# Retention transposes three half units behind the norm, output weights fetched a unit sooner, low parts first in batch 1, x2 stored in column halves

## The chip, the cores and the metric

The kernel runs on one core of a Trainium2 chip. The core has five engines, each with its own instruction stream, run in order: TensorE (PE: matrix products and transposes into PSUM), VectorE (DVE), ScalarE (ACT), GpSimd (POOL) and SyncE (SP), which here issues the DMA transfers between HBM and the on-chip memory. Semaphores tie the streams together. The metric is the time of one execution on the device, in microseconds (us); less is better.

## The reference

One layer of a hybrid encoder runs over two inputs of 512 rows by 1024 columns, "batch 0" and "batch 1" here. Everything is float32:

```python
mod = silu(c) @ w_ada + b_ada                      # sh1, sc1, g1, sh2, sc2, g2
h = rms_norm(x, norm1_g) * (1 + sc1) + sh1
q_a, k_a, v_a, q_r, k_r, v_r, g_r = split(h @ w_in)
o_a = windowed_attention(q_a, k_a, v_a, sink)      # 8 heads of 64, blocks of 128 rows
o_r = bidirectional_retention(q_r, k_r, v_r, g_r)  # 4 heads of 128
x = x + g1 * (concat(o_a, o_r) @ w_out)
h = rms_norm(x, norm2_g) * (1 + sc2) + sh2
x = x + g2 * (square(relu(h @ w_mlp1)) @ w_mlp2)
return rms_norm(x, final_g)
```

Retention normalises each head's output y before it is gated: the mean is taken off, the result is multiplied by 1/sqrt(variance + 1e-6) and by silu(g_r).

## The kernel before

**Precision.** A float32 matrix is split into a high part that TensorE multiplies at full rate and a low part, the rest. A product is three matmuls: high·high, high·low, low·high. The high part is a cast on ScalarE, the low part a subtraction on VectorE. A weight w becomes the tiles `wh_…` and `wl_…`. For batch 0 weights are loaded, split and also written back to HBM (`keep_unit`); batch 1 loads the two parts (`kept_unit`): the high ones into pool `ws`, the low ones of the output weights into pool `ws2`, which has 3 slots and also takes parts of the MLP's weights (`wc_a`, `wc_s`).

**Units.** The work on TensorE is a list of units, one per weight tile. `run_units` loads a unit's weights while the unit before it computes; after each half unit it calls `between(rate)`. This gives the waiting stages (attention blocks, retention heads) `rate` steps of credit. A stage is a generator; `yield n` says that its next step may not come before n half units. Two stages are active at a time.

**Retention.** `ret_head` computes the scores `prs` of a 128-row chunk, multiplies them with the decay mask (`rsf`, VectorE), splits them (`rsc`), and multiplies them with the values into `py`. Then y is transposed into `pyn`, VectorE takes mean and variance (`mv`), `va` = variance + eps (tile `rva`) and `nb` = −mean (`rnb`), GpSimd raises `rva` to −1/2 (`rrs`) and multiplies `rnb` by it, ScalarE writes the normalised `ryn`, and four transposes give `pyb`, which is gated into `mix`.

**Output projection.** `out_units(b)` makes eight units: column half `hf` (512 columns) times four parts `kq` of the inner dimension (two 128-blocks each). A half's four row tiles t build up in four banks `po_b_hf_t`. The mixer's output is split into `ms` when the weights of half 0 are loaded. `mm3_late` takes the products of a unit so that those with the weight's low part come last. At part 3 each row tile is finished by itself: product with the gate row (`go`), addition to x (`x_b_t`); for half 0 of batch 1 the tile of x is loaded there, in program order. After half 1 the row is complete: `store` writes it to `x2s`, `squares` (ScalarE) and `scaled` (VectorE, GpSimd) make the second norm; for batch 1 the last row tile is scaled into two tiles `xl_0`, `xl_1`. `norm2` transposes the scaled rows into `px_b_kc` (the transposes are at line 268). The MLP then follows (`py_…`, `px_…` at line 940 with the weights `wc_…` and the halves of its input `hch`, `hcl`).

**Order around the change.** Batch 1's units (attention, values, four retention heads) run at rate 1.3; then `out_units(0)` by itself at rate 1.0, with its first weights loaded when its first unit begins; then batch 1's output projection beside `norm2` of batch 0 and the first MLP products. A scheduler orders the engines' streams from the recorded program; SyncE's queue is served in order, so a transfer whose semaphore isn't there holds all behind it.

## Time and profile before

| | us |
|---|---|
| median of 3 runs | 1107.09 |
| lowest, highest | 1106.03, 1108.5 |
| profiled execution, its own time | 1107.0 |
| its span | 1105.2 |
| mean granted TensorE clock | 0.998 |

The profile gives, for one execution, when each instruction ran and which semaphore ended a wait. "Busy" matmuls overlap each other, so the duration of one (0.39 us for 512 columns) is longer than the distance from one to the next. An engine that is busy for nearly the whole span sets its length; what the others do matters where that engine waits for them.

### The profile page before, as it was taken

The numbers are of one execution on the slowest core, as the hardware profiler recorded it, in microseconds if no ns is written. First come the engines' busy times: TensorE is split into PE (matmuls) and PEld (weight loads), VectorE is DVE, ScalarE is ACT, GpSimd is POOL, SyncE is SP. The second block draws the span as 40 slices with busy tenths as digits, with TensorE's granted clock in tenths as the row PEclk, the third lists the DMA queues.
The fourth block names the chain that finished last, engine by engine and source line by source line (L and its number), as shares of the span: only waits on it lengthen the run. The fifth ranks groups of instructions, "written<-read, shape, count | busy, mean of one in ns | idle before, by whom it ended". The sixth has DMA issues, their size and how long they took to land.

```text
span 1105.2 us, 14046 instructions
## 1 busy us (share of the span) xinstructions
PE 1081.8 (98%) x5021; PEld 889.3 (80%) x5021; DVE 864.2 (78%) x1448; ACT 516.0 (47%) x885; POOL 53.3 (5%) x63
## 2 busy tenths in 40 slices
PE   8999999999999999999999999999999999999997
PEld 5777887777888787888888888888888888888886
DVE  7979898877885787789778777786759754589786
ACT  6576676545652443474433333333443732335342
POOL 1000000010000001000000000000000000002213
PEclk9999999999999999999999999999999999999999
DMA  9888898855545698633555445552883555525504
GB/s 373 336 303 314 303 346 271 248 179 175 171 156 180 229 362 302 256 146 126 190 181 184 159 152 176 169 190 105 300 325 109 187 192 196 206 77 191 190 20 152
DMA packets 86746, 232.73 MB, mean 211 GB/s; under 512 B 8578, under 2 KB 20882, under 8 KB 86676
## 3 DMA queue, kind: packets, MB, share of 16 engines
q1 hardware_dynamic: 86084, 231.25, 60.3%
q8 instruction: 39, 0.64, 0.2%
q10 hardware_dynamic: 432, 0.57, 0.1%
q14 instruction: 31, 0.25, 0.1%
q0 software_dynamic: 160, 0.02, 0.0%
HBM read 160.75 MB, written 71.06 MB: 210 GB/s over the span
## 4 chain that ended last, share of the span: by engine, by line
PE 82%; DVE 11%; ACT 2%; DMA 2%; issue 1%; POOL 1%; POOLq 0%; DVEq 0%; ACTq 0%
PE x L1357 16%; PE px_None L940 15%; PE y L1357 12%; PE py_None L940 11%; PE po L132 2%; PE po L134 2%; PE po L131 2%; DVE jka_b L178 2%; PE po L396 2%; PE ppt L389 1%; PE psc L360 1%; PE pj_rq L131 1%; PE pj_rq L132 1%; PE pj_rq L134 1%; DVE jka_f L178 1%
## 5 line engine op out<-in xcount | busy, mean ns | idle before, releaser
L1297 DVE TENSOR_TENSOR uc_l<-ur,uc_h 128x1024 fp32r<-128x1024 f32 x56 | 68.4, 1221 | 52.7 <-ACT uc_h L1297 35.5
L1357 PE MATMUL x<-wc_l,uc_h 128*128 128x512 f32 (+1 forms) x264 | 101.0, 383 | 0.0
L1357 PE MATMUL x<-wc_h,uc_l 128*128 128x512 f32 (+1 forms) x264 | 101.0, 383 | 0.0
L1357 PE MATMUL x<-wc_h,uc_h 128*128 128x512 f32 (+1 forms) x264 | 100.9, 383 | 0.0
L1297 ACT CAST uc_h<-ur 128x1024 fp32r<-128x1024 f32 x56 | 58.8, 1051 | 77.1 <-PE x L1357 25.1
L1357 PE MATMUL y<-wc_h,uc_h 128*128 128x512 f32 x192 | 74.7, 389 | 0.0
L1357 PE MATMUL y<-wc_l,uc_h 128*128 128x512 f32 x192 | 74.7, 389 | 0.0
L1357 PE MATMUL y<-wc_h,uc_l 128*128 128x512 f32 x192 | 74.7, 389 | 0.0
L1297 ACT CAST wc_h<-w 128x1024 fp32r<-128x1024 f32 x48 | 50.5, 1051 | 48.1 <-PE x L1357 24.7
L1297 DVE TENSOR_TENSOR wc_l<-w,wc_h 128x1024 fp32r<-128x1024 f32 x48 | 58.6, 1220 | 17.6 <-ACT wc_h L1297 13.6
L1357 PEld LDWEIGHTS x<-wc_h,uc_h 128*128 128x128 f32 x264 | 49.6, 188 | 9.9 <-issue 0.2
L1357 PEld LDWEIGHTS x<-wc_l,uc_h 128*128 128x128 f32 x264 | 49.6, 188 | 9.7
L1357 PEld LDWEIGHTS x<-wc_h,uc_l 128*128 128x128 f32 x264 | 49.6, 188 | 9.6
L131 PE MATMUL po<-wh_wo,ms 128*128 128x512 f32 x128 | 50.3, 397 | 0.0
L132 PE MATMUL po<-wh_wo,ms 128*128 128x512 f32 x128 | 49.8, 392 | 0.1
L178 DVE CUSTOM_DVE_ANT_0 jka_b<-raw_adat,cb,cols 128x1024 bf16<-128x1024 f32 x38 | 48.3, 1280 | 0.2
L845 ACT CAST wc_s4h<-raw_w 128x1024 fp32r<-128x1024 f32 x16 | 16.8, 1052 | 63.1 <-PE px_None L940 44.9
L370 ACT ACTIVATE st<-st,negm 128x256 f32<-128x256 f32 (+1 forms) x64 | 35.2, 554 | 20.1 <-DVE negm L365 20.1
L1357 PEld LDWEIGHTS y<-wc_h,uc_h 128*128 128x128 f32 x192 | 36.0, 188 | 7.5
L1357 PEld LDWEIGHTS y<-wc_l,uc_h 128*128 128x128 f32 x192 | 36.0, 188 | 7.5
L1357 PEld LDWEIGHTS y<-wc_h,uc_l 128*128 128x128 f32 x192 | 36.0, 188 | 7.5
L940 PE MATMUL py_None<-hch,wc_a 128*128 128x512 f32 x120 | 39.7, 389 | 0.0
(379 smaller groups left out, 2963.0 us busy)
## 6 DMA issues: line engine op xcount, KB each, us to landing
ur<-spill SPq DMA_DIRECT2D x56, 512.0 KB, 4.4
raw_adat<-in_w_ada_t_dram SPq DMA_DIRECT2D x36, 512.0 KB, 6.4
raw_w<-in_w_mlp_dram SPq DMA_DIRECT2D x32, 512.0 KB, 3.5
spill<-s SPq DMA_DIRECT2D x64, 256.0 KB, 3.6
w<-in_w_mlp_dram SPq DMA_DIRECT2D x32, 512.0 KB, 5.0
spill<-u SPq DMA_DIRECT2D x48, 256.0 KB, 2.0
raw_ada<-in_w_ada_t_dram SPq DMA_DIRECT2D x12, 512.0 KB, 9.3
x<-in_x_dram SPq DMA_DIRECT2D x12, 512.0 KB, 7.7
```

The source lines that it names most:

```text
L131: nc.tensor.matmul(ps, lhs[0], rhs[0], start=start, stop=False)
L132: nc.tensor.matmul(ps, lhs[late], rhs[1 - late], start=False, stop=False)
L134: nc.tensor.matmul(ps, lhs[1 - late], rhs[late], start=False, stop=stop)
L178: nc.vector.tensor_tensor_reduce(junk(f"jka_{name}_{sec}_{kc}_{b}"), t, cb[:, b, :], 1.0, bcol[:, sec * KC + kc:sec * KC + kc + 1] if bias ...
L360: nc.tensor.matmul(psc[:, :w], qs[hh][:, isl], k_[:, s, j0 * P:j1 * P], start=(s == 0), stop=(s == 1))
L370: nc.scalar.activation(st[hh][:, :w], st[hh][:, :w], AF.Exp, bias=negm[:, hh:hh + 1], scale=0.125, accum_out=den[:, hh:hh + 1])
L389: nc.tensor.transpose(pt[:, hh * P:(hh + 1) * P], st[hh][:, jj * P:(jj + 1) * P], ident)
L396: nc.tensor.matmul(po, va[:, j0 + jj, g].rearrange("p s e -> p (s e)"), pts[jj][:, s, :], start=(jj == 0 and s == 0), stop=(jj == nj - 1 a ...
L845: nc.scalar.copy(hi, src)
L940: self.last = nc.tensor.matmul(bank[:, cs], x[:, k, :], y, start=first and k == 0 and i == 0, stop=last and k == 3 and i == 2, skip_group_ ...
L1297: last_split[:] = [nc.scalar.copy(hi, src), nc.vector.tensor_sub(lo, src, f(hi))]
L1357: nc.tensor.matmul(out, left[n][x][:, i, ts_], right[n][y][:, i, cs], start=first and i == 0 and k == 0, stop=end and i == 1 and k == 2, s ...
```

## The change

The edits are these. `mm3_late` can take the products with the weight's low part first, and does so for batch 1's output projection. In `ret_head`, `nb` is computed ahead of `va`, and the transposes into `pyb` come three half units behind the norm instead of two. `store` takes a column range; batch 1 stores each half of a row as soon as it is added. `out_units(0)` is appended to batch 1's units in one list, so the load of its first weights falls beside the last retention unit, and its half units give 1.3 steps, not 1.0.

```diff
-    def mm3_late(groups, late):
+    def mm3_late(groups, late, low_first=False):
+        def low():
+            for ps, lhs, rhs, start, stop in groups:
+                nc.tensor.matmul(ps, lhs[1 - late], rhs[late], start=start and low_first, stop=stop and not low_first)
+        if low_first:
+            low()
+        for ps, lhs, rhs, start, stop in groups:
+            nc.tensor.matmul(ps, lhs[0], rhs[0], start=start and not low_first, stop=False)
+            nc.tensor.matmul(ps, lhs[late], rhs[1 - late], start=False, stop=stop and low_first)
+        if not low_first:
+            low()
...
         va = small([P, NT], f"rva_{nm}")
-        nc.vector.tensor_scalar(va, mv[:, :, 1], EPS, None, ALU.add)
         nb = small([P, NT], f"rnb_{nm}")
         nc.vector.tensor_scalar(nb, mv[:, :, 0], -1.0, None, ALU.mult)
+        nc.vector.tensor_scalar(va, mv[:, :, 1], EPS, None, ALU.add)
...
-        yield 2
+        yield 3
         pb = aux_bank(f"pyb_{nm}")
...
-        def store(t):
+        def store(t, cs=slice(0, D)):
             r0 = b * S + t * P
-            nc.sync.dma_start(x2s[r0:r0 + P, :], x2[t])
+            nc.sync.dma_start(x2s[r0:r0 + P, cs], x2[t][:, cs])
...
-                               (w[0][:, k, :], w[1][:, k, :]), kq + k == 0, kq + k == 4) for t in ts_ for k in range(2)], 1)
+                               (w[0][:, k, :], w[1][:, k, :]), kq + k == 0, kq + k == 4) for t in ts_ for k in range(2)], 1, b == 1)
...
+                        if b == 1:
+                            store(t, hs)
                         if hf == 1 and b == 1:
-                            store(t)
                             squares(hf, t)
...
-    run_units(units, 1.3)
-    units, norm2_0 = out_units(0)
-    run_units(units, 1.0)
+    more, norm2_0 = out_units(0)
+    run_units(units + more, 1.3)
```

How the streams change at three places. First VectorE at the norm of retention head 2 of batch 0 (`mv_2` is its mean and variance, `jka_b` a piece of the modulation, `qs` the low part of an attention projection). Before:

```order
L453 TENSOR_SCALAR rva_2_2333<-mv_2_2320 128x4
L338 TENSOR_TENSOR qs_0_2306<-pj_q_0_2267,qs_0_2306 64x512
L178 ISA jka_b_6_0_2313,gm<-raw_adat_2218,cb,cols 128x1024
L178 ISA gm 128x1
L455 TENSOR_SCALAR rnb_2_2335<-mv_2_2320 128x4
L178 ISA jka_b_6_1_2362,gm<-raw_adat_2218,cb,cols 128x1024
L178 ISA gm 128x1
L422 SCALAR_TENSOR_TENSOR rsf_3_2_2371<-prs_3_2_2367,dtab_3_2186 128x512
L467 SCALAR_TENSOR_TENSOR mix_3_1841<-pyb_2_2397,rg_2_1838 128x512
```

With the change:

```order
L456 BN_AGGR mv_2_2315<-bn_2_3_2325 128x2
L459 TENSOR_SCALAR rnb_2_2329<-mv_2_2315 128x4
L460 TENSOR_SCALAR rva_2_2328<-mv_2_2315 128x4
L427 SCALAR_TENSOR_TENSOR rsf_3_1_2344<-prs_3_1_2340,dtab_3_2190 128x512
L430 TENSOR_TENSOR rsc_3_1_2346<-rsf_3_1_2344,rsc_3_1_2346 128x512
L183 ISA jka_b_6_1_2366,gm<-raw_adat_2222,cb,cols 128x1024
L183 ISA gm 128x1
L343 TENSOR_TENSOR qs_1_2380<-pj_q_1_2353,qs_1_2380 64x512
```

`rnb_2` stood four rows behind `rva_2`; now the two are neighbours.

Second TensorE at the beginning of batch 0's output projection, which falls beside head 2 of batch 1 (`prs_2_3`: scores of its chunk 3; `py_2<-rsc_2_1`: chunk 1 times its values; `po_0_t`: the projection's banks). Before, from `prs_2_2` on:

```order
L124 MATMUL prs_2_2_3923<-rq_2_3531,rk_2_3602 128x512
L125 MATMUL prs_2_2_3923<-rq_2_3531,rk_2_3602 128x512
L126 MATMUL prs_2_2_3923<-rq_2_3531,rk_2_3602 128x512
L124 MATMUL py_2_3814<-rsc_2_1_3845,rv_1_2868 128x512
L131 MATMUL po_0_0_3904<-wh_wo_0_0_3879,ms_0_0_3883 128x512
L131 MATMUL po_0_1_3905<-wh_wo_0_0_3879,ms_0_0_3883 128x512
L131 MATMUL po_0_2_3906<-wh_wo_0_0_3879,ms_0_0_3883 128x512
L131 MATMUL po_0_3_3907<-wh_wo_0_0_3879,ms_0_0_3883 128x512
L124 MATMUL prs_2_3_3949<-rq_2_3531,rk_2_3602 128x512
L125 MATMUL prs_2_3_3949<-rq_2_3531,rk_2_3602 128x512
```

With the change, the rows that end in the same product:

```order
L136 MATMUL po_0_1_3899<-wh_wo_0_1_3885,ms_1_1_3892 128x512
L137 MATMUL po_0_1_3899<-wh_wo_0_1_3885,ms_1_1_3892 128x512
L132 MATMUL po_0_0_3898<-wl_wo_0_1_3886,ms_1_0_3889 128x512
L132 MATMUL po_0_0_3898<-wl_wo_0_1_3886,ms_1_1_3892 128x512
L132 MATMUL po_0_1_3899<-wl_wo_0_1_3886,ms_1_0_3889 128x512
L132 MATMUL po_0_1_3899<-wl_wo_0_1_3886,ms_1_1_3892 128x512
L124 MATMUL py_2_3845<-rsc_2_1_3880,rv_1_2864 128x512
L125 MATMUL py_2_3845<-rsc_2_1_3880,rv_1_2864 128x512
L126 MATMUL py_2_3845<-rsc_2_1_3880,rv_1_2864 128x512
L124 MATMUL prs_2_3_4003<-rq_2_3526,rk_2_3594 128x512
```

Before, the product with `rsc_2_1` follows the last row of its scores `prs_2_1` after 18 matmuls and four transposes, and another chunk's scores are put between its parts; now 49 matmuls lie between, a whole half unit of the projection among them, and its three parts stand together.

Third SyncE's queue in batch 1's output projection (`x_1_t` is row tile t of x, `wh_wo_1_q` and `wl_wo_1_q` the weights of column half 1, part q, `raw_w` the MLP's weights). Before:

```order
L787 DMA x_1_0_4652<-in_x_dram 128x1024
L787 DMA x_1_1_4657<-in_x_dram 128x1024
L787 DMA x_1_2_4662<-in_x_dram 128x1024
L787 DMA x_1_3_4667<-in_x_dram 128x1024
L119 DMA wh_wo_1_1_4692<-kept_wo_1_4239 128x1024
L119 DMA wl_wo_1_1_4694<-kept_wo_1_4239 128x1024
L119 DMA wh_wo_1_2_4758<-kept_wo_2_4289 128x1024
L119 DMA wl_wo_1_2_4760<-kept_wo_2_4289 128x1024
L876 DMA raw_w_1_0_4921<-in_w_mlp_dram 128x1024
L253 DMA gate_1_512_4762<-gates 128x512
L119 DMA wl_wo_1_3_4809<-kept_wo_3_4353 128x1024
L119 DMA wh_wo_1_3_4807<-kept_wo_3_4353 128x1024
```

With the change:

```order
L740 DMA x2s<-x_1_0_4652 128x512
L792 DMA x_1_1_4658<-in_x_dram 128x1024
L119 DMA wl_wo_1_2_4764<-kept_wo_2_4324 128x1024
L882 DMA raw_w_1_0_4925<-in_w_mlp_dram 128x1024
L740 DMA x2s<-x_1_1_4658 128x512
L792 DMA x_1_2_4664<-in_x_dram 128x1024
L119 DMA wl_wo_1_3_4813<-kept_wo_3_4359 128x1024
L740 DMA x2s<-x_1_2_4664 128x512
L792 DMA x_1_3_4670<-in_x_dram 128x1024
L740 DMA x2s<-x_1_3_4670 128x512
L258 DMA gate_1_512_4766<-gates 128x512
L119 DMA wh_wo_1_3_4811<-kept_wo_3_4359 128x1024
```

The four loads of x stood together; now each of the last three stands behind the half store of the tile before, and the gate row and `wh_wo_1_3` behind all four stores. On TensorE, in the same place, the eight matmuls with `wl_wo_1_3` stood behind the high ones of each tile and are now ahead of them, and 24 rows of the MLP, where there were 8, stand between them and the sixteen with `wh_wo_1_3`.

More of the change, by code (lines that the diff above doesn't have):

```diff
@@ L126, in mm3 @@
         nc.tensor.matmul(ps, lhs[1], rhs[0], start=False, stop=stop)
-    def mm3_late(groups, late):
-        for ps, lhs, rhs, start, _ in groups:
-            nc.tensor.matmul(ps, lhs[0], rhs[0], start=start, stop=False)
-            nc.tensor.matmul(ps, lhs[late], rhs[1 - late], start=False, stop=False)
-        for ps, lhs, rhs, _, stop in groups:
-            nc.tensor.matmul(ps, lhs[1 - late], rhs[late], start=False, stop=stop)
+    def mm3_late(groups, late, low_first=False):
[9 more added lines that the diff above has]
+            low()
     ident = const.tile([P, P], F32, name="ident")
```

## The prediction

> **What bounds the kernel now.** I read the page first: the span, the engines' busy time, and the chain of work that ended last.
>
> ```profile
> span 1105.2 us, 14046 instructions
> PE 1081.8 (98%) x5021; PEld 889.3 (80%) x5021; DVE 864.2 (78%) x1448; ACT 516.0 (47%) x885; POOL 53.3 (5%) x63
> PE 82%; DVE 11%; ACT 2%; DMA 2%; issue 1%; POOL 1%; POOLq 0%; DVEq 0%; ACTq 0%
> ```
>
> TensorE is busy for 1081.8 of 1105.2 us and holds 82% of the chain. The change adds no matmul and takes none away, so it can win only where TensorE stands still and lose only where it will. The profiled execution took 1107.0 us, 1.8 around its span; the median of three runs is 1107.09, so both are the same to 0.1. The order of instructions differs between the two kernels only from TensorE's row for about 172 us to that for about 505 us. The table of busy time by stretch (columns: stretch, its length, then busy time of PE, PEld, DVE, ACT and POOL with their instructions, granted clock, DMA share, GB/s) gives what can be had there:
>
> ```profile
> 172.00:505.00 333.00, 325.85 (x1604) 268.17 (x1603) 266.07 (x579) 164.07 (x343) 18.29 (x25) 1.00 0.64 216
> 246.00:322.00 76.00, 75.61 (x384) 62.24 (x383) 60.85 (x182) 46.35 (x124) 0.00 (x0) 1.00 0.49 159
> 322.00:374.00 52.00, 52.00 (x239) 42.94 (x237) 34.58 (x76) 16.06 (x29) 2.41 (x4) 1.00 0.60 203
> 374.00:380.00 6.00, 4.87 (x19) 3.19 (x18) 6.00 (x12) 2.70 (x5) 0.00 (x0) 1.00 0.40 156
> 460.00:475.00 15.00, 14.29 (x67) 11.73 (x66) 14.52 (x25) 7.84 (x15) 0.00 (x0) 1.00 0.33 117
> 486.30:490.00 3.70, 2.48 (x22) 2.49 (x23) 2.60 (x5) 3.16 (x5) 0.00 (x0) 1.00 0.15 55
> ```
>
> 333.00 less 325.85 is 7.15 us of idle time at full clock, and that, with some slow spacing that counts as busy, is the most the change can win. The waits of TensorE name it (engine, tile, line, releaser: total, times, longest):
>
> ```profile
> PE pyb L466 <- ACT ryn L461: 3.1, 4, 1.3
> PE px L268 <- ACT x L749: 1.4, 1, 1.4
> PE py L124 <- ACT rsc L424: 1.0, 1, 1.0
> PE py L940 <- ACT wc_a L845: 0.7, 1, 0.7
> PE px L268 <- DVE x L751: 0.3, 1, 0.3
> PE ppt L389 <- DVE mx L362: 0.3, 1, 0.3
> ```
>
> **Retention transposes one half unit later, and −mean ahead of the variance.** The timeline at heads 2 and 3 of batch 0 (start, duration, instruction, idle before it and its releaser):
>
> ```profile
> 222.86 0.17 DVE L453 TENSOR_SCALAR rva<-mv 128x4 f32<-128x4 f32 x1
> 223.78 1.29 DVE L178 CUSTOM_DVE_ANT_0 jka_b<-raw_adat,cb,cols 128x1024 bf16<-128x1024 f32 x1
> 224.99 0.17 DVE L455 TENSOR_SCALAR rnb<-mv 128x4 f32<-128x4 f32 x1
> 225.31 1.10 POOL L459 TENSOR_TENSOR rnb<-rnb,rrs 128x4 f32<-128x4 f32 x1 [1.13 <-DVE rnb L455]
> 226.95 0.33 PE L466 MATMUL pyb<-ident,ryn 128*128 128x128 f32 x1 [1.04 <-ACT ryn L461]
> 244.00 1.38 PE L466 MATMUL pyb<-ident,ryn 128*128 128x128 f32 x4 [0.26 <-ACT ryn L461]
> 372.33 0.60 PE L466 MATMUL pyb<-ident,ryn 128*128 128x128 f32 x4
> ```
>
> At head 2 a low part and a modulation step got between the two small VectorE operations: `rnb` came 2.1 us behind `rva`, and GpSimd and ScalarE waited. In the changed order they are neighbours, and the matmuls between `pyn` and `pyb` grow from 27 to 31. The 1.04 us wait goes, with some 0.06 of spacing: 1.1. At head 3 the distance more than doubles; the wait of 0.26 goes, and the four transposes, which took 1.38 us at ScalarE's pace, take 0.60 as they do at 372.33: 1.0 together. **Gain 2.1.** Heads 0 and 1 of batch 0 keep exactly their old matmuls between `pyn` and `pyb`, by the order of both kernels, so the rest of the 3.1 us, 1.28 and 0.49 (1.8), stays. If the new cover failed, the two waits would stay: 0, and above 2.1 there is nothing there to win.
>
> In batch 1, head 3, the transposes slip behind `ms` halves that VectorE makes for the joined output units; one pair costs
>
> ```profile
> 444.92 1.29 DVE L768 TENSOR_TENSOR ms<-mix,ms 128x512 fp32r<-128x512 f32 x2
> ```
>
> and two of these stand ahead of `rnb`. They lie beside 6.1 us of matmuls, against 5.4 before, so between −0.5 and one full pair, 1.3: I take a **loss of 0.3**.
>
> **Output projection of batch 0 joined to batch 1's units.** At its start TensorE waited for the last scores of a chunk:
>
> ```profile
> 373.49 0.40 PE L124 MATMUL prs<-rq,rk 128*128 128x512 f32 x1
> 373.95 0.40 PE L126 MATMUL prs<-rq,rk 128*128 128x512 f32 x1
> 375.38 0.49 PE L124 MATMUL py<-rsc,rv 128*128 128x512 f32 x1 [1.03 <-ACT rsc L424]
> ```
>
> Two steps in 0.46 us make 0.23 for one 512-column matmul. The stretch from 374 to 380 holds 19 of them, 4.3 us of 6.0: 1.7 lost, where the wait itself shows 1.03. Before, the first `py` row for chunk 1 stood 18 matmuls and four transposes (4.5 us of work) behind the last `prs` row of its scores; in the changed kernel it stands 49 matmuls behind (11.3 us). The path between them is a mask product, a cast and a low part on two engines; the smallest such distance anywhere in the changed order is 6.1 us. **Gain 1.7** (bounds 1.0 and 2.0). The weights that are now fetched a unit sooner, and the casts, low parts and `ms` halves that go with them, fall into 322 to 374 us. There VectorE is busy for two thirds of the time and the DMA engines for 0.60; nothing in that stretch waits on either, so I cost the move at nothing. If that cover were gone, a unit's low parts would hold TensorE for one pair, 1.3.
>
> Stages of batch 1 also start sooner. The attention stretch from 246 to 322 us has 0.39 us idle and a 0.3 us wait of `ppt`; by the changed order no score is nearer to its use than 5.5 us. **Gain 0.6**, with bounds −1.0 (the three stalls that the nearer scores could bring, at 0.3) and 1.5. The wait of `px` for batch 0's scaled rows, 0.3, gets 0.9 us more matmuls ahead of it: **gain 0.3**, or none if the stores on which the scaling waits stay late.
>
> **Low parts first and stores by column halves, batch 1.** This is the part that can cost. Rows for the DMAs between 440 and 490 us (tiles, queue, count, size, median us from issue to landing), one from the page for half-size stores, and the end of the stretch in the chain of waits:
>
> ```profile
> x<-in_x_dram SPq DMA_DIRECT2D x4, 512.0 KB, 8.8
> raw_w<-in_w_mlp_dram SPq DMA_DIRECT2D x3, 512.0 KB, 4.1
> x2s<-x SPq DMA_DIRECT2D x4, 512.0 KB, 2.8
> wl_wo<-kept_wo SPq DMA_DIRECT2D x4, 512.0 KB, 7.4
> spill<-u SPq DMA_DIRECT2D x48, 256.0 KB, 2.0
> DMA to landing us min/median/max: 4.7/4.7/4.7
> 453.98 0.68 DVE L790 TENSOR_TENSOR x<-x,go 128x512 f32<-128x512 f32 x1
> 473.76 0.39 PE L940 MATMUL py<-hch,wc_a 128*128 128x256 f32 x1 [0.71 <-ACT wc_a L845]
> 480.04 1.22 DVE L846 TENSOR_TENSOR wc_s4l<-raw_w,wc_s4h 128x1024 fp32r<-128x1024 f32 x1
> 480.00 0.47 PE po L134 x2
> 482.50 3.71 DMA x2s<-x
> 486.31 1.16 ACT x L749
> 487.51 1.09 PE px L268 x8
> 488.61 1.44 PE px L940 x12
> ```
>
> (The row with 4.7 three times is that of `wh_wo_1_3`.) Now SyncE issues the four loads of x in a row; in the changed program each later load stands behind the store of the tile before, and that store waits for VectorE's addition. So loads 1 to 3 run one after the other. With 4.4 us for a load, between the 4.1 of `raw_w` and the 4.7 of `wh_wo` in a stretch whose DMA share is 0.33, a round is 0.4 of issue, 4.4, and 0.7 for the addition: 5.5. The first addition ends at 454.7, so three rounds end the last one at 471.2. VectorE's order puts seven operations of 0.7 and the 1.2 us low part `wc_s2l` behind it: 477.3. TensorE reaches the first matmul that needs it after 8 low matmuls and 14 MLP rows: 473.05 (473.76 less the 0.71) + 8 × 0.23 + 14 × 0.12 = 476.6 (a 256-column matmul is 1.44/12). So a stall of 0.7 to 0.8 takes the place of the 0.7 for `wc_a`. `wh_wo_1_3` is queued behind the same stores and the gate: issued at about 472.1, there 4.7 later at 476.8, wanted ten MLP rows behind `wc_s2l` at 478.5, covered by 1.7.
>
> Then the ending. 24 rows of the MLP, not 8, now stand ahead of `wh_wo_1_3`'s matmuls, so the last of those 16 ends at 478.5 + 16 × 0.23 = 482.2 instead of 480.47, and 24 rows instead of 40 are left to cover the last tiles' way through addition, store, norm and scaling. The tiles follow each other in 0.91 us (4 matmuls) instead of 1.36 (6), which makes VectorE queue them. Tile 2's bank is full at 481.3; tile 1's product and sum, the 1.22 us `wc_s4l` and its own product and sum go first, so its addition ends at 484.4, its half store takes about 2.3 instead of 3.71, ScalarE's scaling 1.16: 487.9. Tile 3 is added by 487.1; its squares come behind that scaling on ScalarE, and it is scaled by 489.9, so the group that began at 488.61 begins at about 490.5. **Loss 2.0.** Low end 0.5 (loads at 3.5 or less leave VectorE alone as the bound, and the half store ends sooner by 1.7), high end 4 (each load 0.7 slower). The low weights are wanted first now: 7.4 us to land lies within a unit of 48 matmuls, 10.9 us, so they cost nothing.
>
> [...]
>
> **Sum.** −2.1 + 0.3 − 1.7 − 0.6 − 0.3 + 2.0 = −2.4; 1107.0 − 2.4 = **1104.6**.
>
> **The rivals.** *The ending gives most of it back.* Batch 0's gain at `px` is lost to its stores, and the ending costs 4, not 2: 1107.0 − 2.1 − 1.7 − 0.6 + 0.3 + 4.0 = 1106.9. For it: 2.7 of the 7.15 idle us lie in these two last stretches already, where VectorE is busy for 14.52 of 15 us. Against it: the half store shortens the longest link.
>
> *Slower: the loads of x in series.* If each takes what the row of x shows now, 8.8 us, rather than 4.4, three rounds end 13.2 us later, at 484.4, and `wc_s2l`, the gate and `wh_wo_1_3` with it. `wc_s2l` has no cover, so each us is one of TensorE: at 6.5 us a load it comes 3 × 2.1 = 6.3 later and the time is 1110.9; at 8.8 it is 1117.8. It decides from about 6 us a load (3 × 1.6 = 4.8, which makes 1109.4). Against it: those 8.8 us belong to four loads in flight beside three weight tiles, with the DMA engines nearly full; one alone finds them less loaded.
>
> *More.* If loads land in 3.5 us or less, as the page's `raw_w` do, VectorE alone sets the last addition; with the half store the ending costs 0.5 or less, and attention gives its 1.5: 1102.2. [...]
>
> *The third half unit does nothing.* Its effect on heads 0 and 1 is nil by the order. If heads 2 and 3 also kept their waits, with ScalarE as the pace and not the small operations, 2.1 would stay: 1106.7.
>
> **How the numbers follow.** Forecast 0.50, with its own range 1103 to 1106; the ending gives it back 0.15; slower 0.14; more 0.16; no effect at the transposes 0.05. A measurement of this kernel tells about 0.2%, 2.2 us, from no change: faster lies below 1104.9. Of the forecast 0.32 falls below that, with "more" 0.48; the remaining 0.18 with the two small cases makes 0.38 the same; 0.14 slower. The range 1101.5 to 1108.8 leaves out most of the slower case and a little below.
>
> **What would show it.** Right: waits of `pyb` fall from 3.1 to about 1.8 with the 1.28 and 0.49 of heads 0 and 1 left; no wait of `py` for `rsc`; a new wait of `py` for `wc_s2l` near 476 and a longer one of `px` for x; loads of x some 5.5 us apart. Wrong: loads over 6 us (slower), or `px` without a longer wait (more). A new wait inside attention, or for the weights of the first output units, would break the terms that I set at 0.6 and at nothing.

## The result: 1% slower, and the profile after

| | runs | median us | lowest to highest |
|---|---|---|---|
| before | 6 | 1106.78 | 1105.42 to 1108.5 |
| changed | 6 | 1117.77 | 1114.82 to 1119.44 |

The ratio is 1.0097 (95% interval 1.0081 to 1.0113): the changed kernel is slower by about 11 us, and the forecast of 1104.6 with its range to 1108.8 did not hold it. The profiled execution took 1117.76 us. First its page, then TensorE's waits from 172 to 515 us (engine, tile, line, releaser: total, times, longest):

```profile
span 1116.0 us, 14040 instructions
PE 1085.6 (97%) x5021; PEld 894.7 (80%) x5021; DVE 864.4 (77%) x1448; ACT 517.0 (46%) x885; POOL 56.9 (5%) x63
```

```profile
PE pyb L471 <- ACT ryn L466: 4.0, 3, 2.2
PE px L273 <- ACT x L754: 2.7, 2, 1.9
PE psc L365 <- ACT ryn L466: 1.9, 1, 1.9
PE py L946 <- ACT wc_s2h L851: 1.0, 1, 1.0
PE py L946 <- DVE wc_s2l L852: 0.9, 1, 0.9
PE px L273 <- DVE xl L752: 0.8, 1, 0.8
```

TensorE executes the same 5021 matmuls, and yet is busy for 3.8 us longer. The waits that the change was to remove are gone or shorter (`py` for `rsc` from 1.0 to 0.2, `wc_a` from 0.7 to nothing), but there are four new ones: `psc` for `ryn`, `wc_s2h`, `wc_s2l` and `xl`. The waits of 0.2 us and more add up to 12.1 us where they were 6.9. Span less busy time grew from 23.4 to 30.4 us: 7.0 us more in which TensorE stood still, of which these waits are 5.2. With the 3.8 us of longer busy time that is the whole difference of the spans, 10.8 us.

To see where the time was lost, follow three instructions that both programs execute at the same place of the work: the power of the variance of retention head 0 of batch 1, the fourth row piece `hr` of batch 0's second norm, and the first sum of an MLP product behind the ending of the output projections. Start, duration, instruction, before:

```profile
354.44 1.01 POOL L457 TENSOR_TENSOR rrs<-rva,neghalf 128x4 f32<-128x4 f32 x1 [110.98 <-DVE rnb L455]
...
451.29 0.81 DVE L823 TENSOR_SCALAR hr<-px,mod_a,mod_s 128x512 f32<-128x512 f32 x1 [2.81 <-PE px L268]
...
514.62 0.69 DVE L968 TENSOR_TENSOR s<-u,u 128x512 f32<-128x512 f32 x1
```

and in the changed kernel:

```profile
355.03 1.01 POOL L462 TENSOR_TENSOR rrs<-rva,neghalf 128x4 f32<-128x4 f32 x1 [104.65 <-DVE rva L460]
...
453.10 0.81 DVE L829 TENSOR_SCALAR hr<-px,mod_a,mod_s 128x512 f32<-128x512 f32 x1 [2.80 <-PE px L273]
...
524.90 0.68 DVE L974 TENSOR_TENSOR s<-u,u 128x512 f32<-128x512 f32 x1
```

The lag is 0.59 us at the first, 1.81 at the second and 10.28 at the third. (At 177 us, at the last `mv` ahead of every moved instruction, it is 0.17 already, 177.22 and 177.05, which comes from the start of the program.) So the heads of batch 0 with batch 1's attention gave +0.4 where I had put −2.7, the stretch to 451 us gave +1.2 where I had −1.7, and the ending of the output projections gave **+8.5** where I had +2.0. Between the second and the third instruction TensorE stood still for 5.5 us where it was 2.1 (3.4 more), and was busy for 66.3 us where it was 61.2 (5.1 more).

**The ending.** SyncE's queue in batch 1's output projection (start, duration of the issue, line, transfer):

```profile
456.88 0.43 SPq L792 DMA_DIRECT2D x<-in_x_dram  x1
...
462.51 0.32 SPq L740 DMA_DIRECT2D x2s<-x  x1
462.88 1.32 SPq L792 DMA_DIRECT2D x<-in_x_dram  x1
...
468.19 0.32 SPq L740 DMA_DIRECT2D x2s<-x  x1
468.56 0.42 SPq L792 DMA_DIRECT2D x<-in_x_dram  x1
...
474.77 0.32 SPq L740 DMA_DIRECT2D x2s<-x  x1
```

and the chain of waits of the same execution there (start, duration, piece):

```profile
462.88 4.56 DMA x<-in_x_dram
...
467.47 0.70 DVE x L795
...
468.56 5.46 DMA x<-in_x_dram
...
479.32 1.15 DVE wc_s2l L852
...
480.51 2.50 PE py L946 x10
```

The series is there: load, addition, half store, next load. The chain that ended last runs through it, and then through VectorE's queue up to `wc_s2l`, for which TensorE waits. That is the mechanism that the prediction described; its length is the question of the section behind the experiments.

**The clock.** The stretches of TensorE's busy time (columns: stretch, length, busy time of PE, PEld, DVE, ACT, POOL with their instructions, granted clock, DMA share, GB/s), cut at the places where the granted clock changes:

```profile
418.96:422.37 3.41, 1.40 (x7) 0.82 (x5) 3.41 (x6) 0.35 (x1) 2.95 (x2) 1.00 0.98 306
422.38:425.78 3.40, 3.25 (x9) 2.37 (x10) 1.46 (x3) 1.15 (x4) 0.00 (x0) 0.50 0.55 195
476.99:480.40 3.41, 1.59 (x12) 1.19 (x10) 3.34 (x5) 2.32 (x3) 0.00 (x0) 1.00 0.66 174
480.41:483.81 3.40, 3.30 (x13) 3.10 (x14) 0.05 (x1) 0.00 (x0) 0.00 (x0) 0.50 0.54 180
490.64:494.05 3.41, 1.48 (x11) 1.00 (x10) 1.99 (x5) 1.83 (x4) 0.65 (x1) 1.00 0.57 223
494.06:500.87 6.81, 5.97 (x27) 5.57 (x28) 4.71 (x9) 3.32 (x7) 0.54 (x1) 0.50 0.03 9
```

Three times the granted clock falls from 1.00 to 0.50, for 3.4, 3.4 and 6.8 us, and each time the 3.41 us ahead of it have TensorE busy for less than half: 1.40, 1.59, 1.48. At half clock a matmul takes longer and counts as busy for longer: the 256-column rows of the MLP follow each other there in 0.21 us (480.89, 481.11, 481.32) and have durations of 0.41, where the prediction's rows gave 0.12 and the kernel before has 0.28. That is the busy time that was to be explained: at most half of 13.6 us, 6.8. All stretches lie on one grid of 3.41 us: the falls at 422.38, 480.41 and 494.06 are 58.03 and 13.65 us apart, 17 and 4 times 3.413, and the clock records of this trace hold no level but 1.00 and 0.50. In the profile of the kernel before, no wait lowered it between 12 and 1100 us: it is 1.00 throughout.

A busy time of less than half does not settle whether the clock falls. In e1_heads, below, a stretch of 3.41 us has 1.50 us busy, and the clock stays at full in the one behind it:

```profile
248.55:251.96 3.41, 1.50 (x9) 1.07 (x7) 2.97 (x10) 1.54 (x5) 1.73 (x2) 1.00 0.66 208
251.97:255.37 3.40, 3.40 (x16) 2.92 (x17) 1.65 (x6) 0.53 (x1) 0.00 (x0) 1.00 0.66 242
```

In e7_fill it stays at full behind 1.42 us (490.54 to 493.95), and in e9_all_loads_first it falls to 0.50 behind 2.01 (422.11 to 425.52). What decides is open.

How much time the low clock cost can be read from the executions of the changed kernel. One of the six had a mean granted clock of 0.997 and took 1114.82 us; the other five had 0.990 to 0.992 and took 1117.37 to 1119.44. By that one execution the low clock is worth about 3 of the 11 us, and about 8 are there without it.

### The profile page after: what moved, and what is told of

Its sections match the earlier page's. It is cut to its first block, busy times and chain, and to the rows that moved or that the text cites. A ratio compares the mean times of both kernels' runs of the same rounds, so it can differ in the third digit from the quotient of the medians.

```text
span 1116.0 us, 14040 instructions
## 1 busy us (share of the span) xinstructions
PE 1085.6 (97%) x5021; PEld 894.7 (80%) x5021; DVE 864.4 (77%) x1448; ACT 517.0 (46%) x885; POOL 56.9 (5%) x63
## 4 chain that ended last, share of the span: by engine, by line
PE 78%; DVE 15%; DMA 2%; ACT 2%; issue 2%; POOL 1%; SPq 0%; POOLq 0%; DVEq 0%; ACTq 0%
PE x L1362 16%; PE px_None L946 15%; PE y L1362 12%; PE py_None L946 11%; DVE jka_b L183 2%; PE po L401 1%; PE psc L365 1%; PE po L136 1%; PE po L137 1%; PE ppt L394 1%; PE po L132 1%; DVE jka_f L183 1%; PE pj_rv L136 1%; PE pj_rk L136 1%; PE pj_rq L136 1%
## 5 line engine op out<-in xcount | busy, mean ns | idle before, releaser
L1362 PEld LDWEIGHTS x<-wc_h,uc_h 128*128 128x128 f32 x264 | 49.6, 188 | 10.8 <-ACT adacc L251 1.2
```

The lines of the kernel that those rows point to most:

```text
L1362: nc.tensor.matmul(out, left[n][x][:, i, ts_], right[n][y][:, i, cs], start=first and i == 0 and k == 0, stop=end and i == 1 and k == 2, s ...
```

## The experiments

Fourteen kernels, in the order of the questions. "Before" was run beside each group: 1106.65 us (first four), 1107.36 (next four), 1106.52 (next four), 1106.82 (last two). "Lag" is against the kernel before, at the three instructions above.

| kernel | median us | ratio (95%) | lag at 354, 451, 515 |
|---|---|---|---|
| e1_heads | 1113.49 | 1.0063 (1.0048 to 1.0078) | 0.6, 4.7, 4.7 |
| e2_join | 1110.51 | 1.0039 (1.0026 to 1.0052) | −0.7, 3.2, 3.3 |
| e3_low | 1105.47 | 0.9991 (0.9981 to 1.0) | −0.6, −1.7, −2.6 |
| e4_halves | 1112.3 | 1.0052 (1.0037 to 1.0067) | 0.0, 0.2, 4.7 |
| e5_low_halves | 1113.87 | 1.0058 (1.0043 to 1.0073) | 0.0, −0.4, 6.8 |
| e6_no_halves | 1109.72 | 1.002 (1.001 to 1.003) | 2.1, 2.4, 1.5 |
| e7_fill | 1116.81 | 1.0083 (1.0068 to 1.0098) | 0.6, 1.9, 8.1 |
| e8_loads_first | 1105.9 | 0.9985 (0.9976 to 0.9995) | −0.6, −1.5, −2.6 |
| e9_all_loads_first | 1110.97 | 1.0043 (1.003 to 1.0057) | 1.5, 3.3, 3.4 |
| e10_third_only | 1113.11 | 1.0063 (1.005 to 1.0075) | 2.1, 7.2, 7.5 |
| e11_swap_only | 1109.54 | 1.0025 (1.0015 to 1.0035) | 2.3, 1.1, 3.1 |
| e12_low_first_swap | 1107.72 | 1.0008 (0.9998 to 1.0018) | 2.9, 2.5, 1.4 |
| e13_one_head | 1105.31 | 0.9986 (0.9977 to 0.9995) | −1.1, −1.9, −3.0 |
| e14_one_head_join | 1113.66 | 1.006 (1.0046 to 1.0074) | −1.4, 2.8, 7.1 |

The lag is that of one profiled execution and carries from −0.7 to 0.2 us from the program's start.

### Each part alone: e1_heads, e2_join, e3_low, e4_halves

The kernel before with one part of the change each: the swap and the third half unit; the joined list; the low parts first; the half stores.

```diff
 e1  -        yield 2
     +        yield 3                        # and nb ahead of va
 e2  -    run_units(units, 1.3)
     -    units, norm2_0 = out_units(0)
     -    run_units(units, 1.0)
     +    more, norm2_0 = out_units(0)
     +    run_units(units + more, 1.3)
 e3  ...
     -    ... for t in ts_ for k in range(2)], 1)
     +    ... for t in ts_ for k in range(2)], 1, b == 1)
 e4  ...
     +    if b == 1:
     +        store(t, hs)
      if hf == 1 and b == 1:
     -        store(t)
```

The dots stand for lines left out: the definition of `mm3_late` in e3 and that of `store` in e4 are those of the whole change.

> Only the retention edit: -mean ahead of the variance, transposes three half units behind. In the changed kernel head 3 of batch 0 let TensorE wait 1.9 us for ryn at 252 us (a psc row now stands behind pyb's work), and head 3 of batch 1 waited 2.2 us at 422 us, behind which the granted clock was 0.55 to 0.59 for about 3.5 us. Theory A (these waits come from the third half unit itself): both waits are there without the other edits, time about 1107.0 - 2.1 + 1.9 + 2.2 + 1.7 = 1110.7. Theory B (the wait at 422 needs the joined units, which bring casts and low parts of ms and wl_wo between the norm and the transposes): only the wait at 252 is left, time 1106.5 to 1107, clock 1.00 near 425.

> Only the joined output units at rate 1.3. Prediction's terms for it: the 1.03 us wait of py for rsc goes (-1.7), stages sooner (-0.6 of which a part), so about 1105 with no new wait over 0.5 us and clock 1.00 from 360 to 440. Theory A' (the joined units alone load VectorE so that pyb of head 3 waits even with two half units): a wait of 2 us or more at 415 to 425, a low clock behind it, 1108 or more.

> Only the low parts first in batch 1's output projection; the four loads of x stand together in SyncE's queue as before. Theory L (the rows of the MLP moved ahead of the last projection unit leave too few to cover the last tiles): waits of px for x of 2 us or more near 490, a low clock behind, 1109 to 1112. Theory S (the loads of x in series are what costs): no wait for wc_s2l, the ending as before or better, 1106.5 to 1107.5.

> Only the stores by column halves; the loads of x stand one behind each half store. Theory S: waits for wc_s2h, wc_s2l or the weights of the last projection unit near 475 to 480 and for x near 490, a granted clock of 0.5 to 0.6 for some 3.5 us behind one or both, 1111 to 1115. Theory L: the loads alone cost at most 1.5, 1107 to 1108.5, clock 1.00.

Three of the four parts cost time by themselves, 0.39 to 0.63%, and only the low parts first take some away, 0.09% with an interval that touches no change. Their sum would be 1.45%, the change has 0.97%: parts take each other's waits away and bring others. In time, e2 came out as its theory A' and e4 as its theory S; e3 was 1 us better than its theory S, and e1 slower than both of its theories: the wait at 252 us is there and the one at 422 is not, but TensorE lost 4 us at a place where neither looked. e2's waits were of 1.3 and 1.4 us, though, and not of 2, and e4's profile has no low clock (1.00 in every stretch from 172 to 530 us).

In e1_heads the timeline shows a wait that the prediction has nowhere, at the start of batch 0's output projection:

```profile
376.92 0.62 ACT L424 CAST rsc<-rsf 128x512 fp32r<-128x512 f32 x1 [3.80 <-DVE rsf L422]
...
377.44 2.17 ACT L767 CAST ms<-mix 128x512 fp32r<-128x512 f32 x4
...
378.11 1.96 PE L131 MATMUL po<-wh_wo,ms 128*128 128x512 f32 x4 [4.03 <-ACT ms L767]
```

The casts of `ms` stand behind that of `rsc` in ScalarE's stream, `rsc` waits 3.80 us for VectorE's `rsf`, and TensorE stands still for 4.03. In the kernel before, the casts of `ms` stand behind one of `rsc` too (374.71), but that one waited 1.15 only. In e1 `rsf` comes at 376.19, behind a low part, the gating of `rg` and a `jka_b` on VectorE. e10, below, has the same wait without the swap. In e2_join the wait for `rsc` is gone, as forecast, and the transposes `pyb` of heads 2 and 3 of batch 1 wait 1.3 and 1.4 us instead; the granted clock is 0.91 from 400 to 420 us and 1.00 in the stretches around that. In e4_halves the loads of x stand in series, TensorE waits 0.7 and 1.3 us for `wc_a`, 0.5 for `wh_wo` and 2.1 for `px`; some of each were there before (0.7 for `wc_a`, 1.4 for `px`). The clock stays at full in this profile. From 451 to 515 us it lost 4.5 us: TensorE stood still for 3.2 us more and was busy for 1.3 more, with the same 363 matmuls.

### The ending: e5_low_halves, e6_no_halves, e7_fill, e8_loads_first, e9_all_loads_first

e5 has the low parts first and the half stores, e6 all of the change but the half stores. e7 is the changed kernel with 40 transposes of the identity put where TensorE waits for `pyb` of head 3 and for `px`; what they write is overwritten. e8 is e5 with the four loads of x issued together, ahead of the first half store; e9 is the whole change with that. The diff shows one of e7's two places and e8's whole edit against e5.

```diff
 e7  +    if b == 1 and h == 3:
     +        for _ in range(16):
     +            nc.tensor.transpose(pb[:, :P], ident, ident)
 e8  +    for t in range(NT) if hf == 0 else ():
     +        x2[t] = x2_tile(t)
     +        tc.keep_in_program_order(nc.sync.dma_start(x2[t], xin[b][t * P:(t + 1) * P, :]))
          for t in range(NT):
     -        if hf == 0:
     -            x2[t] = x2_tile(t)
     -            tc.keep_in_program_order(nc.sync.dma_start(x2[t], xin[b][t * P:(t + 1) * P, :]))
```

> Low parts first and stores by halves together, the heads and the joined units left as before. In the changed kernel the shift against before grows by 8.5 us between 451 and 515 us; low parts first alone gave -0.9 there and the halves alone +4.5. Theory I (the two edits make the ending bad together: the loads of x in series come later than the moved rows of the MLP, and the low parts first take cover away): +7.5 to +8.5, 1114 to 1115, with waits for wc_s2h or wc_s2l and for x and at least one stretch of low clock behind them. Theory P (the excess over the sum is the low clock, which falls where a wait happens to fill one of its windows of 3.413 us, and the order itself adds nothing): 1110 to 1112 if no window falls, some 1.7 more for each that does.

> The changed kernel with whole stores after half 1, so the loads of x stand together; heads, joined units and low parts first are kept. If the halves make the ending's cost, the shift at 451 us stays as in the changed kernel (+1.8) and the ending gives -0.9: 1107 to 1108, with the wait of pyb near 422 left (2 us and a window of low clock) and none for wc_s2h or wc_s2l. If heads and joined units cost in the ending too: 1111 or more.

> The changed kernel with 40 transposes of the identity added, 16 ahead of the pyb transposes of head 3 of batch 1, and 16 and 8 among the px transposes of batch 1; they write places that the real transposes overwrite. They take about 0.11 us each, inside the waits of 2.2, 1.9 and 0.8 us. Theory C (the low clock comes from TensorE standing still for most of a 3.413 us window, and then costs half of the next window): the low stretches at 422 and 494 to 501 are gone or halved although the waits for ryn and x end when they did: 1117.5 - 1.7 - 1.7 to 3.4 = 1112.5 to 1114, clock 1.00 there. Rival W (only the waits count, the clock falls with the order or by chance): 1117 to 1119, low stretches as before.

> Low parts first and stores by halves, but the four loads of x are issued together ahead of the first addition, so that no load waits for a store. If the series of loads is the whole cost of the halves: the last addition of half 0 is back near 459 us, no wait for wc_s2l, and the shorter last store takes up to 1 us off the wait of px for x: 1104.5 to 1105.5 (low parts first alone: 1105.5). If the half stores themselves cost (more transfers beside the weights): 1107 or more.

> The changed kernel with all its parts, but the four loads of x of batch 1 issued together ahead of the first half store. If the loads in series are the only thing that the column halves cost, this comes to the changed kernel without the halves or a little under it, 1108 to 1110 us, and the wait of py for the low part of wc_s2 near 480 us is gone. If the half stores or the denser row of waits in the ending cost something of their own once the output units are joined, it stays at 1112 or above.

**The series is the cost of the halves.** From the second instruction to the third, e5 loses 7.2 us and e8, with the loads together, wins 1.1, as much as e3 without any half store (0.9). In the whole change the series costs 6.0 us (e9: 1.0097 less 1.0043), and the halves with their series 8.5 (e6: less 1.002). Low parts and halves together show a longer lag than halves alone (e5 6.8, e4 4.7), although their waits near 480 are no longer: the mean granted clock is 0.995 in e5's profile and 0.998 in e4's, by an estimate from these and the span some 6.7 us more at half clock. Their ratios (1.0058 and 1.0052) are not distinct. e5 came out at its theory I (7.2 where 7.5 to 8.5 was expected). e8 and e9 came out near what was expected of the series alone (1105.9, where 1105.5 was the upper end, and 1110.97, where 1110 was); e6 was 1.7 us above its 1108, but its ending gave the −0.9 that was forecast.

**Half stores are not free where something urgent is behind them.** e9 is slower than e6 (1.0043, from 1.003 on, against 1.002, up to 1.003; the intervals just touch). Its timeline shows a wait that e6 has not (SyncE's issue, and TensorE's wait):

```profile
460.43 0.92 SPq L740 DMA_DIRECT2D x2s<-x  x2
461.40 0.45 SPq L119 DMA_DIRECT2D wl_wo<-kept_wo  x1
```

```profile
467.37 1.20 PE L132 MATMUL po<-wl_wo,ms 128*128 128x512 f32 x4 [1.89 <-DMA wl_wo<-kept_wo]
```

A low weight, wanted first now, is queued behind half stores that wait for additions; it is issued at 461.40, lands 5.92 us later by the chain of waits, and TensorE waits 1.89 us. In e14_one_head_join, below, the same wait is 3.8. In e8, where the output units are not joined, it is not there. The clock falls twice in e9's profile (at 251.45 and 425.53 us, mean 0.995), and by an estimate from the mean, 0.996, once in e6's, which can hold up to 1.7 us of the difference.

**The clock costs less than its 13.6 us suggest.** In e7's profile the granted clock stays at full through the whole middle (mean 0.999, where the changed kernel has 0.992), and the time falls by 1 us only (1117.77 to 1116.81; the ratios' intervals overlap), where 3.5 to 5 had been expected. The clock stays up near 480 us too, where nothing was filled in, and behind the 1.42 us busy from 490.54 on, so the run does not prove that the filling kept it up. The reason stands in the rows of ScalarE's scaling of row tile 2 and of the `px` behind it, in e7_fill:

```profile
492.79 1.15 ACT L760 ACTIVATE x<-x,r 128x1024 f32<-128x1024 f32 x1 [2.51 <-DMA x2s<-x]
...
493.99 0.33 PE L276 MATMUL px<-ident,x 128*128 128x128 f32 x1 [2.03 <-ACT x L760]
```

and in the changed kernel:

```profile
492.86 1.15 ACT L754 ACTIVATE x<-x,r 128x1024 f32<-128x1024 f32 x1 [0.95 <-DMA x2s<-x]
...
494.06 1.11 PE L273 MATMUL px<-ident,x 128*128 128x128 f32 x4 [1.95 <-ACT x L754]
```

Without the slow stretch at 480 us the same work was done 1.6 us sooner, but tile 2's scaling began at the same moment in both, because it waits for the tile's half store to land: ScalarE's wait grew from 0.95 to 2.51. So the low clock ahead of 494 us was hidden in a wait, and only what came behind it can have cost: by the lags at 515 us, 2.2 us, with the 0.9 us of the last eight filling transposes in it. The half store was issued 1.6 us sooner in e7 and took 4.4 us to land, where it took 2.8 in the changed kernel; why was not tried.

### The heads and the joining: e10_third_only to e14_one_head_join

e10 has the third half unit alone, e11 the swap alone, e12 is e8 with the swap, e13 is e8 with the third half unit at head 2 of batch 0 only, e14 is e13 with the joined list.

```diff
 e10 -        yield 2
     +        yield 3
 e11 -nc.vector.tensor_scalar(va, mv[:, :, 1], EPS, None, ALU.add)
      nb = small(...); nc.vector.tensor_scalar(nb, mv[:, :, 0], -1.0, None, ALU.mult)
     +nc.vector.tensor_scalar(va, mv[:, :, 1], EPS, None, ALU.add)
 e13 -        yield 2
     +        yield 3 if (b, h) == (0, 2) else 2
```

> Only the third half unit (yield 3), variance and mean in the old order. If the third half unit is what hurts, by holding the bank of pyn for longer so that psc waits for ryn near 252 us, that wait of about 1.9 us is here too, and the time is near 1113 as with both edits. If it was the swap of the two small operations (GpSimd's power beside VectorE), the wait of psc is not here and the time is 1105 to 1107.

> Only the swap: mean ahead of variance, two half units as before. If the third half unit is what hurts, no wait of psc for ryn appears, the wait of pyb of 1.04 us at head 2 shrinks by what the 2.1 us between the two operations cost it, and the time is 1105.5 to 1107. If the swap hurts, it is above 1109.

> What is left of the change when the two parts that cost are taken away: low parts first, half stores with the four loads of x together, and the swap; no third half unit, output units not joined. If the parts add, this is the low parts with the loads together (1105.9) less the wait of head 2, about 1105, faster than both kernels. If the swap alone does nothing, it stays at 1105.9; if a small shift of the streams brings new waits, it is above 1107.

> Low parts first, half stores with the four loads of x together, and the third half unit at head 2 of batch 0 alone, the one place where it took a wait away; no swap, output units not joined. If what the third half unit costs sits at head 3 (psc waiting for ryn near 252 us) and in batch 1 (po waiting for ms near 378 us), neither wait is here, pyb does not wait near 227 us, and the time is 1104.5 to 1105.5, a little under the 1105.9 without it. If a third half unit anywhere moves the stages so that other waits come, it is above 1107.

> The same with the output units of batch 0 joined. If joining costs by itself, by the nearness of the transposes pyb to ryn at heads 2 and 3 of batch 1 and by late low weights, it is 3 to 5 us above the run without the joining, 1108 to 1110. If joining only cost because of the third half unit, it is at or under the run without it, 1103 to 1105.5.

The third half unit alone has the ratio of e1, and both its waits (`psc` 1.98, `ms` 4.03): it is the costly half. But the expectation for the swap failed too: 1109.54, where 1105.5 to 1107 was to come. In e11_swap_only the wait of `pyb` at head 2 did not shrink; it doubled, from 1.04 to 2.08:

```profile
222.24 0.17 DVE L454 TENSOR_SCALAR rnb<-mv 128x4 f32<-128x4 f32 x1
...
224.38 0.17 DVE L455 TENSOR_SCALAR rva<-mv 128x4 f32<-128x4 f32 x1
224.45 1.28 DVE L178 CUSTOM_DVE_ANT_0 jka_b<-raw_adat,cb,cols 128x1024 bf16<-128x1024 f32 x1
...
224.69 1.91 POOL L457 TENSOR_TENSOR rrs<-rva,neghalf 128x4 f32<-128x4 f32 x1 [24.57 <-DVE rva L455]
...
227.42 0.41 PE L466 MATMUL pyb<-ident,ryn 128*128 128x128 f32 x1 [2.08 <-ACT ryn L461]
```

The swap by itself does not make the two small operations neighbours. The scheduler still puts a low part and a modulation step between them, and now it is `rva`, ahead of the power, that comes 2.1 us late. The power then runs beside the next `jka_b` and takes 1.91 us. In e10, without the swap, the two are neighbours, as in the changed kernel: the third half unit did that. e12 has the same wait of 2.06 us at head 2 and is slower than e8 by 0.2% (1107.72; 1105 was expected if the parts add).

e13 shows what the heads were worth. With the third half unit at head 2 only, neither the `psc` nor the `ms` wait is there, `pyb` waits 1.7 us in all (two times), and the lag at the first instruction is −1.1, the term of 1.1 that the prediction had for head 2. Its ratio, 0.9986 (0.9977 to 0.9995), is the best with e8: some 1.5 us under the kernel before, and not distinct from e8's, so that the 1.1 shows in one profile and not in the median times.

e14 isolates the joining: on that same base it costs 8 us (1105.31 to 1113.66; 3 to 5 were expected), on the kernel before it cost 4 (e2); the changed kernel without it was not run. In e14 it acts through the `pyb` waits of heads 2 and 3 of batch 1 (1.3 and 1.4), the late `wl_wo` (3.8) and a lower granted clock (mean 0.995, where e13 has 0.999).

## Why the prediction was wrong, point by point

**The loads of x in series: right mechanism, as the slower rival had it, and mis-sized in the sum.** The forecast priced a round at 5.5 us and the last addition at 471.2; the rival was to decide from 6 us a load. The loads took 4.2, 4.6 and 5.5 us to land, under that bound, and yet the ending cost 8.5. The term of 2.0 was wrong in three places. First, the rounds: the additions end at 456.48 and 474.73, so the three rounds took 6.0, 5.7 and 6.6 us, 18.25 and not 16.5: the last load was 1.1 longer than the 4.4 I took, and in the first round the addition waited 0.7 for VectorE. That is 1.7. Second, from the last addition to the group of MLP products that the forecast set at 490.5, I counted 19.3 us, and it took 22.05 (it began at 496.78): the waits for `wc_s2h` and `wc_s2l`, 1.9 us, where one of 0.8 was expected, and a stretch of 3.4 us at half clock from 480.41 on, which can hold up to 1.7. The half store of tile 2, which was to take 2.3 us, took 2.8 and was the last thing that its scaling waited for (492.86), but the tile's scale factor (`r`) was ready only at 492.42, so a shorter store would have won 0.4 at most. Third, the half clock: the 4.1 us from 496.78 to 500.87 did half their work, 2.0. With the lag of 1.8 taken off, the group came 6.4 us later than before and the clock added 2.0: 8.4 of the 8.5. So no single load was slow. Several errors, each small, came in series on a path with no cover. The "more" case, with loads that land in 3.5 us or less, was not to be had here: these took 4.2 to 5.5. One reading of the rows in that part was off and carried no term: the 2.7 us of idle time that the first rival put into the last two stretches are 1.93 by its own rows (0.71 and 1.22).

**Heads 2 and 3 of batch 0: what was forecast to go went, and a wait on another tile came.** `pyb` of both heads no longer waits. But head 3's norm, from the transposes `pyn` to ScalarE's `ryn`, moved and grew. Before:

```profile
238.97 0.60 PE L446 MATMUL pyn<-ident,ryt 128*128 128x128 f32 x4
...
243.49 1.50 ACT L461 ACTIVATE ryn<-pyn,rnb,rrs 128x128 f32<-128x128 f32 x4 [1.31 <-POOL rnb L459]
```

and in the changed kernel, with the matmul that waited:

```profile
243.53 0.60 PE L451 MATMUL pyn<-ident,ryt 128*128 128x128 f32 x4
...
248.02 1.99 POOL L462 TENSOR_TENSOR rrs<-rva,neghalf 128x4 f32<-128x4 f32 x1 [3.02 <-DVE rva L460]
...
250.41 1.50 ACT L466 ACTIVATE ryn<-pyn,rnb,rrs 128x128 f32<-128x128 f32 x4 [4.50 <-DVE mod_a L212]
...
251.97 0.62 PE L365 MATMUL psc<-ks,qs 128*128 128x384 f32 x2 [1.90 <-ACT ryn L466]
```

Scores of batch 1's attention (`psc`) wait until ScalarE has read `pyn`. Both take their banks from the same pool of five (`aux_bank`), and head 3's norm held its bank from 243.53 to 251.91, for 8.4 us, where it was 6.0; that this pool is the reason was argued from the code and from the releaser in the row, and not tried with another pool. In the code the third half unit stands behind the reading of `pyn`, so the delayed transposes do not hold that bank themselves. With the third half unit at every head, head 3's norm began 4.6 us later (4.9 in e10, which has nothing else changed), among other work of VectorE, and GpSimd's power took 1.99 us and not 1.03. In e13, with the third half unit at head 2 only, the norm of head 3 takes 5.2 us (238.19 to 243.43) and `psc` does not wait.

So two steps failed. One is "above 2.1 there is nothing there to win" and "0 if the cover fails": the bound of zero below had no reason. The other is the gain of 0.6 in attention, whose lower bound looked at when a score is used and not at when its bank comes free. The prediction had named the sign for it, a new wait inside attention, and this is one. e13 fits the 1.1 for head 2; the 1.0 for head 3 was paid back with 1.9. The credit that I gave to the neighbours `rnb` and `rva` belongs to the third half unit, as e10 and e11 show.

**Head 3 of batch 1: a loss of 0.3, within −0.5 and 1.3, was 2.17 us of wait and a stretch at half clock.** The changed kernel there:

```profile
418.24 0.17 DVE L460 TENSOR_SCALAR rva<-mv 128x4 f32<-128x4 f32 x1
...
418.55 3.05 POOL L462 TENSOR_TENSOR rrs<-rva,neghalf 128x4 f32<-128x4 f32 x1 [16.38 <-DVE rva L460]
...
422.02 1.50 ACT L466 ACTIVATE ryn<-pyn,rnb,rrs 128x128 f32<-128x128 f32 x4 [4.20 <-POOL rnb L464]
...
422.53 1.52 PE L471 MATMUL pyb<-ident,ryn 128*128 128x128 f32 x4 [2.17 <-ACT ryn L466]
```

The order of VectorE was right, but GpSimd's power had no term; here it took 3.05 us, three times the 1.01 of the row at 354 us. I had bounded the wait by VectorE's work alone, although two of the eight powers in the profile before took 1.92 and 1.98 us already.

**The joining: the wait for `rsc` went, as forecast, and the term was still wrong in sign.** The "gain of 1.7" holds for 374 to 380 us: TensorE is busy for the whole 6.00 us there, in the changed kernel and in e2. What the earlier stages brought `pyb` at heads 2 and 3 of batch 1, and the low weights, was priced at "nothing", since "nothing in that stretch waits on either"; the waits came 20 to 90 us behind that stretch: at 400 and 425 in e2 and e14, at 422 in the changed kernel, and in e9 and e14 near 468.

**What the profile was to show.** Of the five signs for a right forecast four came: almost no wait for `rsc` (0.2, twice), one for `wc_s2l` (at 480.5, where 476 was named), a longer one of `px` for x (2.7 in all, from 1.4), and loads of x 5.7 to 6.0 us apart. The fifth, `pyb` down to 1.8, did not: 4.0. So most of the signs could not tell this result from the forecast. I had named loads over 6 us as the sign for slower; they stayed below, and the kernel is slower.

**Low parts first: right, and better than their price.** Alone they won 1 us (e3), and the wait for `wc_a` is gone. That the low weights "cost nothing" holds only while no half store is queued ahead of them (waits of 1.89 us in e9 and 3.8 in e14).

**The clock was not in the sum at all.** A wait of 2 us was priced at 2 us. In this kernel it can, by an estimate, cost up to 1.7 more, half of the stretch, for each 3.41 us that follow at half clock; the runs do not show how to tell beforehand whether one follows.

## What to carry to other kernels

On a kernel with an engine at 98%, a gain of 1 us per removed wait is easily lost: ask of each delayed stage which later stages it moves, what those hold for longer (a bank, a slot, a place in an in-order queue), and put a price on that too. Do not let a load stand behind a store of the same queue if that store waits for the load before: that series cost 6.0 us here. With the loads issued together, half stores cost nothing that could be measured (e8 against e3, 1105.9 and 1105.47), unless something urgent was queued behind them (e9, a wait of 1.89 us). And if several estimates lie in series on one path without cover, their errors add; the range has to carry their sum and not the largest.

## What the hardware showed that I had not expected

- Behind waits that left TensorE busy for 1.40 to 1.59 us of one 3.41 us grid stretch, the granted clock was at half for the next 3.41 us (6.8 behind the one at 494 us). But 1.42 us (e7_fill) and 1.50 (e1_heads) lowered nothing, and 2.01 (e9_all_loads_first) did, so the busy time that the profile gives, in which transposes at ScalarE's pace count as busy (1.38 us for four at 244.00 in the kernel before, 0.60 at 372.33), gives no threshold. Nearly the same `psc` wait of 1.9 us lowered the clock to 0.50 in the profile of e9_all_loads_first (1.51 us busy from 248.03 to 251.44) and not in those of e1_heads (1.50) and the changed kernel (1.78 from 248.29 to 251.71).
- GpSimd's power of 4 numbers in 128 rows took 1.01 to 1.03, 1.38 (e2_join), 1.84 to 1.99, or 3.05 us, with different work of VectorE beside it: at 418.55 low parts with two operands (1.22 us, and 1.29 for two), then a `jka_b` of 1.28. That this work made it longer was not shown: no run here took it away.
